# Ten gate tiles of the long sequence as seven-product Strassen groups in a stage of their own, and branch B's later queries and keys drawn over all units

## The chip, the cores and the metric

The kernel runs on one core of a Trainium2 chip, in one launch. The metric is the device time of that core in microseconds (us). Five engines work side by side, each through its own queue of instructions in a fixed order: PE (TensorE, matmuls, with PEld for its weight loads), DVE (VectorE), ACT (ScalarE), POOL (GpSimd), and SP, which only issues DMAs. An instruction that has to wait holds everything behind it on its engine.

## The reference

One layer of an encoder is computed for two inputs, a short one of 512 tokens and a long one of 1024 tokens, each of width 1024. In short:

```python
def _token_mixer(xn, w_in, q_norm_g, k_norm_g, rpb, w_proj_a, w_proj_b, w_out):
    z = xn @ w_in
    qa, ka, va, qb, kb, vb, ga, gb = jnp.split(z, idx, axis=-1)
    ...
    o_a = _gqa_attention(qa, ka, va)
    o_b = _neighbourhood_attention(qb.reshape(...), kb.reshape(...), vb.reshape(...), rpb)
    merged = jax.nn.sigmoid(ga) * (o_a @ w_proj_a) + jax.nn.sigmoid(gb) * (o_b @ w_proj_b)
    return merged @ w_out

def _trunk(x, ...):
    h = h + _token_mixer(_rmsnorm(h, norm_mix_g[l]), ...)
    hn = _rmsnorm(h, norm_mlp_g[l])
    h = h + jnp.square(jax.nn.relu(hn @ w_mlp_up[l])) @ w_mlp_down[l]
    return _rmsnorm(h, norm_final_g)
```

`ga` and `gb` are the two gates, each 1024 columns wide; they are what the change computes in another way. Everything is fp32.

## The kernel before

A product of two fp32 matrices is made of three matmuls: each operand is split into a high part (a copy in the type fp32r, by ACT) and a low part (what is left, a subtraction by DVE), and `mm3` (lines 191 to 193) adds high by high, high by low and low by high. The function `run` goes through one sequence; it is called for the short one (NB = 1, one block of 512 tokens) and then for the long one (NB = 2). Names in the profile have buffer numbers left out; `s1` in a name of the program's order is the long sequence. After both comes the MLP, which the change leaves as it is.

`run` has these stages. For each of two groups g of four heads of branch A: the phase `phR`, which makes queries, keys and values, and the phase `phA`, attention over eight units (a head and a block of 512 queries). In a unit, for each of eight blocks `kc` of 128 keys, PE transposes four tiles of probabilities (`pTs`, line 722), ACT and DVE split them (`pths` line 727, `ptls` line 728), and PE adds them to the output (`os`, lines 698 and 699) two blocks later. Between these, `s_tile` makes the next unit's scores: two times two matmuls into `ss`, a maximum by DVE (`nms`, line 682), an exponential by ACT (`ps`, line 685), a reciprocal by DVE (line 687) and the scaling by POOL (line 688). Then the phase `phB`, branch B: 32 units (a head and a strip of columns), each of `s_unit` (scores `sbs`, the sum with the bias and the minimum by DVE in line 891, exponential, reciprocal, POOL's scaling in line 899), one unit later `t_unit` (transposes `ptbs`, their split), and one more later `v_unit` (`obs`). Then `phG` merges and projects.

The gates are work that can stand anywhere. The generator `gate` makes them in tiles of 128 columns: per tile and block of 512 tokens eight times `mm3`, then a tanh by ACT and a store to `zg` in memory. `fill.pull(n)` takes n steps (one `mm3` each) of whatever `fill` holds, and stands at many places of `phA` and `phB`. For the long sequence, four tiles of the first gate (columns 2304 on) are drawn in each of the two `phA`, with a step in six of eight `kc`, and all eight tiles of the second gate (columns 3328 on) in `phB`, with five or six steps a unit. In `phB`, `qkproj` makes queries and keys for two heads; those of the first pair stand ahead of the units, those of each later pair (96 matmuls) are made within the last two of every eight units.

What is written here is the program's order. A scheduler then sets the order on each engine within what the dependences allow, except where an instruction is kept in program order (`keep_in_program_order`). Buffers come from pools: `rawp` has three of 4 KB per partition for what is loaded or waits to be split, `s8r` eleven of 8 KB, `pmm` four PSUM banks and `pbig` two double ones. A new tile waits until the buffer that it gets was read for the last time.

Of the kernel before, what the change touches and what calls it, by code (L numbers as in the profile page):

```python
# [61 lines left out]
def encoder(ctx: ExitStack, tc: tile.TileContext, xs, outs, w):  # L62
# [316 lines left out]
    def run(tr, nxt, first):  # L379
# [89 lines left out]
        def load_v(g, alloc, pin=False):  # L469
            return load_cols(win, 1792 + 256 * g, 256, f"v{N}_{g}", alloc, pin)  # L470

        early = {}
        for g in range(2):
            with phase(f"phR{N}_{g}") as ph:
                xn_of = {}
                fresh = g == 0 and tr.ready < NT
# [105 lines left out]
                for tt in range(NT):  # L582
# [84 lines left out]
            with phase(f"phA{N}_{g}") as ph:  # L667
# [41 lines left out]
                for ui, u in enumerate(units):  # L709
                    h, qb = u  # L710
                    if first:
                        bias_row(g * 4 + ui)
                        if g == 0 and ui == 1:
                            early["a"] = load_a(1)
                        if g == 0 and ui == 2:
                            early["v"] = load_v(1, slot)
                    nxt_u = units[ui + 1] if ui + 1 < len(units) else None
                    sdone = 0
                    for kc in range(NT):
                        pt = mm(f"pT{N}_{g}_{h}_{qb}_{kc}")  # L720
                        for j in range(4):
                            nc.tensor.transpose(  # L722
                                pt[:, j * P : (j + 1) * P], PP[u, j][:, kc * P : (kc + 1) * P], ident
                            )
                        hi = ph.tile([P, 512], F32R, tag="pth", name=f"pth{N}_{g}_{h}_{qb}_{kc}", bufs=3)
                        lo = ph.tile([P, 512], F32R, tag="ptl", name=f"ptl{N}_{g}_{h}_{qb}_{kc}", bufs=3)
                        nc.scalar.activation(hi, pt, AF.Copy)  # L727
                        nc.vector.tensor_tensor(lo, pt, hi.bitcast(F32), op=ALU.subtract)  # L728
# [9 lines left out]
                fill.drain()  # L738
                for item in queue:
                    pv(*item)  # L740

        mA = {}
        wp_b = []
# [44 lines left out]
        with phase(f"phB{N}") as ph:  # L788
# [18 lines left out]
            def load_qk(pr):  # L807
# [2 lines left out]
                    load_cols(win, 1280 + pr * P, P, f"bk{N}_{pr}"),  # L810
                )

            def qkproj(pr, wqk, dest):
                wq, wk = wqk
                qT = slot([P, 2, T], F32R, f"qB{N}_{pr}")
# [2 lines left out]
                for tb in range(NB):  # L818
                    cs = slice(tb * 512, tb * 512 + 512)
                    pq = mm(f"pqb{N}_{pr}_{tb}")  # L820
                    for k in range(NC8):
                        mm3(pq, wq[k][0], wq[k][1], xh(tb, k), xl(tb, k), k == 0, k == NC8 - 1)
                        yield
                    for e in range(2):
                        hs = slice(64 * e, 64 * e + 64)
                        ls = slice(64 - 64 * e, 128 - 64 * e)

                        src = pq[hs].rearrange("p (r j c) -> p j r c", j=4, c=16)

                        def strip_view(s_):  # L830
                            return qT[s_, e, :].rearrange("p (j r c) -> p j r c", j=4, c=16)[
                                :, :, tb * 8 : tb * 8 + 8, :
                            ]

                        dst_h, dst_l = strip_view(hs), strip_view(ls)
                        nc.scalar.activation(dst_h, src, AF.Copy, scale=0.125)
                        for jj in range(4):
                            nc.vector.scalar_tensor_tensor(
                                dst_l[:, jj],
                                src[:, jj],  # L840
                                0.125,
                                dst_h[:, jj].bitcast(F32),
                                op0=ALU.mult,
                                op1=ALU.subtract,
                            )
# [4 lines left out]
                    for e in range(2):  # L850
                        hs = slice(64 * e, 64 * e + 64)
                        ls = slice(64 - 64 * e, 128 - 64 * e)
                        for os_ in (hs, ls):
                            nc.scalar.activation(kT[e][os_, 0, cs], pk[hs], AF.Copy)
                        for os_ in (hs, ls):
                            nc.vector.tensor_tensor(
                                kT[e][os_, 1, cs], pk[hs], kT[e][hs, 0, cs].bitcast(F32), op=ALU.subtract
                            )

            qk = {}  # L860
            def s_unit(u):
# [86 lines left out]
                    finish_o(o, nq, None, ph, f"B{nm}", (hi, lo, ps))  # L948

            prep(0)  # L950
            fill.add(gate(3328, zg[1]))
            wqk = load_qk(0)
            fill.pull(1)
            for _ in qkproj(0, wqk, qk):
                pass
# [3 lines left out]
            qp = None  # L959
            for i in range(n + LS + LV):  # L960
                if i < n - 8:
                    f = (5 if i < LS else 2 + i % 2) if NB == 1 else 5 + (i % 3 > 0)
                else:
                    f = 3 + i % 2 if NB == 1 else 7
                if i < n:
                    s_unit(units[i])
                    if units[i][1] == 1 and units[i][0] + 1 < 8:
                        prep(units[i][0] + 1)
                    if i % 8 == 6 and i + 2 < n:
# [4 lines left out]
                    if i % 8 == 7 and qp is not None:  # L974
# [11 lines left out]
                if i == n - 8:  # L986
                    fill.drain()
                    fill.add(pa)
                if i == 3:
                    wqk = load_qk(1)  # L990
                if qp is not None and NB == 2:
                    for _ in range(NC8):
                        next(qp)
                fill.pull(f - f // 2)
                if 0 <= i - LS - LV < n:
                    v_unit(units[i - LS - LV])
            fill.drain()


# [707 lines left out]
```

## Time and profile before

| what | value |
|---|---|
| time, median of 3 runs | 2174.46 us (2173.92 to 2176.43) |
| span of the profiled execution | 2172.2 us; its time with what lies around the span is not on the page |
| median run less that span | 2.3 us |
| granted TensorE clock, mean | 0.997 |
| long sequence, `phA` of g = 0 and of g = 1 | about 468 to 592 us and 664 to 788 us |
| long sequence, `phB` up to the last eight units | 790 to 1010 us |

Times of the trace count from the start of the span. The busy time of an engine in a stretch is given beside the number of instructions that lie in it; PE's matmuls overlap each other, so the time that one costs is read from how many fit into a stretch, not from its own duration. A row of groups gives the line, engine, operation, tiles and shapes, the count, and then the busy time in us, the mean duration in ns and the idle time before.

### The profile page before, as it was taken

How to read it: one execution, taken by the hardware profiler on the slowest of the kernel's cores; microseconds unless marked ns; L12 is line 12 of the kernel's file. 1: busy time of each engine (PE TensorE's matmuls, PEld its weight loads, DVE VectorE, ACT ScalarE, POOL GpSimd, SP SyncE). 2: the span in 40 equal slices, each digit the busy share in tenths (PEclk: the TensorE clock that was granted, in tenths of full speed). 3: DMA queues.
4: the chain of work that ended last, by engine and by line, in shares of the span. 5: the costliest groups of instructions: out<-in, count | busy, mean ns of one | idle time of the engine just before them, and what ended most of it. 6: DMA issues, size and time to landing. Idle time of an engine off the chain costs nothing. (4 is left out here: it accounts for less than half of the span.)

```text
span 2172.2 us, 32392 instructions
## 1 busy us (share of the span) xinstructions
PE 2135.6 (98%) x11162; PEld 1867.9 (86%) x11162; DVE 1456.1 (67%) x2837; ACT 1109.3 (51%) x2379; POOL 349.4 (16%) x458
## 2 busy tenths in 40 slices
PE   8999999999999999999999999999999999999998
PEld 7788778888898888888888899998999988888886
DVE  6675566777756754555772777778777777769663
ACT  5654553556645744545531466656556643433452
POOL 2232210433233313322300200003000000000000
PEclk9999999999999999999999999999999999999999
DMA  5436457620122132423464656568544799788551
GB/s 166 144 104 179 137 145 249 211 71 28 45 75 86 44 92 88 125 80 110 136 195 137 202 180 195 179 226 223 158 156 155 234 347 343 224 268 290 175 194 68
DMA packets 319773, 350.94 MB, mean 162 GB/s; under 512 B 31352, under 2 KB 255224, under 8 KB 319609
## 3 DMA queue, kind: packets, MB, share of 16 engines
q1 hardware_dynamic: 277927, 279.65, 41.4%
q10 hardware_dynamic: 36002, 52.19, 6.9%
q0 software_dynamic: 5680, 17.04, 2.7%
q8 instruction: 88, 1.44, 0.3%
q14 instruction: 76, 0.62, 0.1%
HBM read 264.85 MB, written 87.88 MB: 162 GB/s over the span
## 5 line engine op out<-in xcount | busy, mean ns | idle before, releaser
L192 PE MATMUL dn<-wd,ah 128*128 128x512 f32 x624 | 243.0, 389 | 0.0
L193 PE MATMUL dn<-wd,al 128*128 128x512 f32 x624 | 243.0, 389 | 0.0
L191 PE MATMUL dn<-wd,ah 128*128 128x512 f32 x624 | 243.0, 389 | 0.0
L1184 ACT ACTIVATE ah<-ar 128x512 fp32r<-128x512 f32 x168 | 103.9, 627 | 195.1 <-PE dn L192 176.8
L1185 DVE TENSOR_TENSOR al<-ar,ah 128x512 fp32r<-128x512 f32 x168 | 115.1, 693 | 73.9 <-ACT ah L1184 66.7
L192 PEld LDWEIGHTS dn<-wd,ah 128*128 128x128 f32 x624 | 117.2, 188 | 24.4
L193 PEld LDWEIGHTS dn<-wd,al 128*128 128x128 f32 x624 | 117.2, 188 | 24.2
L191 PEld LDWEIGHTS dn<-wd,ah 128*128 128x128 f32 x624 | 117.2, 188 | 24.1
L728 DVE TENSOR_TENSOR ptls<-pTs,pths 128x512 fp32r<-128x512 f32 x160 | 107.7, 686 | 37.9 <-ACT pths L727 37.0
L727 ACT ACTIVATE pths<-pTs 128x512 fp32r<-128x512 f32 x160 | 94.1, 597 | 74.0 <-PE pTs L722 71.8
L688 POOL TENSOR_SCALAR ps<-ps,rls 128x1024 f32<-128x1024 f32 (+1 forms) x96 | 96.6, 1007 | 216.2 <-DVE rls L687 197.2
L682 DVE TENSOR_REDUCE nms<-ss 128x1 f32<-128x1024 f32 (+1 forms) x96 | 99.9, 1041 | 25.4 <-PE ss L680 25.0
L191 PE MATMUL gpss<-xs_0h,w_gs 128*128 128x512 f32 x256 | 106.2, 415 | 0.8 <-DVE rlbs L898 0.7
L685 ACT ACTIVATE ps<-ss,nms 128x1024 f32<-128x1024 f32 (+1 forms) x96 | 93.2, 972 | 22.4 <-DVE nms L682 20.0
L722 PEld LDWEIGHTS pTs<-ident,ps 128*128 128x128 f32 x640 | 78.2, 140 | 28.1 <-POOL ps L688 4.2
L193 PE MATMUL gpss<-xs_0h,w_gs 128*128 128x512 f32 x256 | 101.7, 397 | 0.0
L192 PE MATMUL gpss<-xs_0l,w_gs 128*128 128x512 f32 x256 | 101.6, 397 | 0.0
L722 PE MATMUL pTs<-ident,ps 128*128 128x128 f32 x640 | 98.9, 274 | 1.3 <-DVE ptls L728 0.6
L176 POOL TENSOR_TENSOR rs_f<-ms_f,mhalf 128x1 f32<-128x1 f32 x6 | 4.0, 667 | 590.7 <-DVE ms_f L172 590.7
L1184 ACT ACTIVATE A<-S 128x512 fp32r<-128x512 f32 x128 | 75.9, 623 | 29.4 <-DVE S L1247 22.1
L891 DVE CUSTOM_DVE_ANT_0 sbss<-sbs,bms 128x384 f32<-128x384 f32 (+1 forms) x96 | 48.6, 508 | 58.2 <-issue 34.1
L191 PE MATMUL ud<-B,A 128*128 128x384 f32 x256 | 85.8, 335 | 1.4 <-DVE c L1302 1.4
(325 smaller groups left out, 6444.8 us busy)
## 6 DMA issues: line engine op xcount, KB each, us to landing
ar<-ud SPq DMA_DIRECT2D x120, 512.0 KB
br<-in_w_mlp_down_dram SPq DMA_DIRECT2D x72, 512.0 KB
rawu<-in_w_mlp_up_dram SPq DMA_DIRECT2D x64, 512.0 KB
ud<-c ACTq DMA_DIRECT2D x128, 192.0 KB
raw_gs<-in_w_in_dram SPq DMA_DIRECT2D x32, 512.0 KB
zgs<-sgs ACTq DMA_DIRECT2D x48, 256.0 KB
ud<-cs SPq DMA_DIRECT2D x64, 192.0 KB
raw_os<-in_w_out_dram SPq DMA_DIRECT2D x16, 512.0 KB
```

Of the source, the lines that this page charges most:

```text
L191: nc.tensor.matmul(out, ah, bh, start=start, stop=False, **kw)
L192: nc.tensor.matmul(out, ah, bl, start=False, stop=False, **kw)
L193: nc.tensor.matmul(out, al, bh, start=False, stop=stop, **kw)
L682: nc.vector.tensor_reduce(nm_, s, axis=AX.X, op=ALU.max, negate=True)
L685: nc.scalar.activation(p, s, AF.Exp, bias=nm_, accum_out=l)
L688: nc.gpsimd.tensor_scalar(p, p, rl, 1.0, op0=ALU.mult, op1=ALU.mult)
L722: nc.tensor.transpose(pt[:, j * P : (j + 1) * P], PP[u, j][:, kc * P : (kc + 1) * P], ident)
L727: nc.scalar.activation(hi, pt, AF.Copy)
L728: nc.vector.tensor_tensor(lo, pt, hi.bitcast(F32), op=ALU.subtract)
L891: nc.vector.tensor_tensor_reduce(out=sb, in0=so, in1=bm, op0=ALU.add, op1=ALU.min, scale=-1.0, scalar=3e38, accum_out=nm_)
L1184: nc.scalar.activation(hi, src, AF.Copy)
L1185: nc.vector.tensor_tensor(lo, src, hi.bitcast(F32), op=ALU.subtract)
```

## The change

Three things are changed, all for the long sequence alone.

First, ten of the sixteen gate tiles go into a stage `wide` (phase `phS`) between the second `phA` and `phB`. They are taken as five groups of two tiles. A group is a product of a 1024 x 256 piece of the weights and the 1024 x 1024 input, cut into two by two blocks each, and made by Strassen's scheme (Winograd's form) of seven block products instead of eight; a block product is twelve matmuls of 128x512. Each group needs sums and differences of its weight blocks (`forms`), and all groups share sums and differences of the input's blocks (`x_forms`: numbers 2, 1, 3 and 6 are new; 0, 4, 5 and 7 are the input's own tiles). The new ones are made in 16 parts of 128x512 (`chunk`): POOL subtracts the low halves, DVE the high halves, POOL adds the two, and in a later step (`rest`) ACT makes the high part and DVE the low part. Of the 16 parts, seven stand in units 0 to 6 of the second `phA`, five in unit 7, four in `wide`.

Second, six gate tiles stay with `gate`: two in the first `phA` (a step in two of eight `kc`), three in the second (three of eight `kc`), one in `phB`.

Third, `qkproj2` makes the queries and keys of the pairs 1 to 3 in steps drawn over all eight units before they are needed (`nqp` steps a unit), with its weights asked for earlier.

```diff
+        def x_forms():
+            (h1, l1), (h2, l2) = tr.xhl[0], tr.xhl[1]
+            XF[0], XF[5], XF[4], XF[7] = (h1[0], l1[0]), (h1[1], l1[1]), (h2[1], l2[1]), (h2[0], l2[0])
+            def chunk(i, a, b, c):
...
+                hi, lo = (t[:, c, :] for t in XF[i])
+                (ah, al), (bh, bl) = ([t[:, c, :].bitcast(F32) for t in XF[n]] for n in (a, b))
+                de = rawp.tile([P, 2, 512], F32, tag="raw", name=f"xd{N}_{i}_{c}")
+                pin = tc.keep_in_program_order
+                pin(nc.gpsimd.tensor_tensor(de[:, 1], al, bl, op=ALU.subtract))
+                pin(nc.vector.tensor_tensor(de[:, 0], ah, bh, op=ALU.subtract))
+                pin(nc.gpsimd.tensor_tensor(de[:, 0], de[:, 0], de[:, 1], op=ALU.add))
+                def rest():
+                    pin(nc.scalar.activation(hi, de[:, 0], AF.Copy))
+                    pin(nc.vector.tensor_tensor(lo, de[:, 0], hi.bitcast(F32), op=ALU.subtract))
+                x_rest.append(rest)
+            for i, a, b in ((2, 7, 0), (1, 4, 2), (3, 4, 7), (6, 5, 1)):
+                x_todo.extend(partial(chunk, i, a, b, c) for c in range(4))
...
+        def wide(ph):
+            todo = [(2304 + i * P, i, zg[0]) for i in (4, 6)] + [(3328 + i * P, i, zg[1]) for i in (2, 4, 6)]
...
+                def prod(out, i, more):
+                    for k in range(4):
+                        mm3(out, A[i][:, 0, k, :], A[i][:, 1, k, :], XF[i][0][:, k, :], XF[i][1][:, k, :], ...)
...
+            ask(0)
+            side = forms(0, A)
+            ask(1)
+            for s in side[:3]:
+                s()
+            x_form_step()
+            for s in side[3:]:
+                s()
+            x_form_step()
+            fill.drain()
+            for n in range(len(todo)):
...
+                group(n, A, side)
+                A = nA
+                ask(n + 2)
...
-                        fill.add(gate(2304, zg[0], g * 4, g * 4 + 4))
+                        if NB == 1:
+                            fill.add(gate(2304, zg[0], g * 4, g * 4 + 4))
+                        else:
+                            fill.add(gate(2304, zg[0], g * 2, g * 2 + 2))
+                            if g == 1:
+                                fill.add(gate(3328, zg[1], 0, 1))
...
-                        fill.pull(1 if NB == 1 or kc % 4 < 3 else 0)
+                        fill.pull(1 if NB == 1 or kc % (4 - g) == 0 else 0)
+                        if NB == 2 and g == 1:
+                            if ui < 7:
+                                if kc == 6:
+                                    x_form_step()
+                                if kc == 1 and x_rest:
+                                    x_rest.pop(0)()
+                            elif kc % 2 == 1 or kc == 0:
+                                x_form_step()
...
+        if NB == 2:
+            with phase(f"phS{N}") as ph:
+                wide(ph)
...
+                nqp = (2, 4, 5, 5, 4, 4, 4, 4)[t8] if NB == 2 and i < n - 8 else 0
                 if i < n - 8:
-                    f = (5 if i < LS else 2 + i % 2) if NB == 1 else 5 + (i % 3 > 0)
+                    f = (5 if i < LS else 2 + i % 2) if NB == 1 else (4 if i < 2 else 2)
...
+                for _ in range(nqp // 2):
+                    next(qp, None)
                 fill.pull(f // 2)
                 if 0 <= i - LS < n:
                     t_unit(units[i - LS])
```

What the change does to the order is shown at three places. The first is DVE in the last unit (head 3, block 1) of the long sequence's second `phA`; `ptls` are the low parts that the output's matmuls wait for. Before:

```order
L728 TENSOR_TENSOR ptls1_1_3_1_2_9143<-pTs1_1_3_1_2_9137,pths1_1_3_1_2_9142 128x512
L728 TENSOR_TENSOR ptls1_1_3_1_3_9158<-pTs1_1_3_1_3_9152,pths1_1_3_1_3_9157 128x512
L728 TENSOR_TENSOR ptls1_1_3_1_4_9169<-pTs1_1_3_1_4_9163,pths1_1_3_1_4_9168 128x512
L728 TENSOR_TENSOR ptls1_1_3_1_5_9183<-pTs1_1_3_1_5_9177,pths1_1_3_1_5_9182 128x512
L728 TENSOR_TENSOR ptls1_1_3_1_6_9197<-pTs1_1_3_1_6_9191,pths1_1_3_1_6_9196 128x512
L728 TENSOR_TENSOR ptls1_1_3_1_7_9211<-pTs1_1_3_1_7_9205,pths1_1_3_1_7_9210 128x512
```

And now, with `xds` the differences (line 487) and `xfls` the low parts (line 492) of the new input forms, whose high parts and sums come from ACT and POOL:

```order
L492 TENSOR_TENSOR xfls1_3_8972<-xds1_3_0_8973,xfhs1_3_8971 128x512
L487 TENSOR_TENSOR xds1_3_1_9010<-xs1_1h1_4989,xs1_1h0_4988 128x512
L895 TENSOR_TENSOR ptls1_1_3_1_4_9022<-pTs1_1_3_1_4_9016,pths1_1_3_1_4_9021 128x512
L895 TENSOR_TENSOR ptls1_1_3_1_5_9033<-pTs1_1_3_1_5_9027,pths1_1_3_1_5_9032 128x512
L492 TENSOR_TENSOR xfls1_3_8972<-xds1_3_1_9010,xfhs1_3_8971 128x512
L487 TENSOR_TENSOR xds1_3_2_9038<-xs1_1h1_4989,xs1_1h0_4988 128x512
L895 TENSOR_TENSOR ptls1_1_3_1_6_9050<-pTs1_1_3_1_6_9044,pths1_1_3_1_6_9049 128x512
L895 TENSOR_TENSOR ptls1_1_3_1_7_9064<-pTs1_1_3_1_7_9058,pths1_1_3_1_7_9063 128x512
L492 TENSOR_TENSOR xfls1_3_8972<-xds1_3_2_9038,xfhs1_3_8971 128x512
L487 TENSOR_TENSOR xds1_3_3_9069<-xs1_1h1_4989,xs1_1h0_4988 128x512
```

Two instructions of a form now stand ahead of every two `ptls`, and the first of them needs POOL's and ACT's part of the same form.

The second place is POOL from the last unit on. Before, its last scaling of branch A is followed by branch B's mask and bias sums:

```order
L688 TENSOR_SCALAR ps1_1_3_1_2_9026<-ps1_1_3_1_2_9026,rls1_1_3_1_2_9029 128x1024
L688 TENSOR_SCALAR ps1_1_3_1_3_9050<-ps1_1_3_1_3_9050,rls1_1_3_1_3_9053 128x1024
L790 DMA msks1_9238<-in_mask2_dram 128x2304
L874 TENSOR_TENSOR bms1_0_1_0_9417<-rects1_0_9240,msks1_9238 128x384
L874 TENSOR_TENSOR bms1_0_1_1_9430<-rects1_0_9240,msks1_9238 128x384
```

Now ten parts of the input's forms (number 1 from its third part, then 3 and 6), two instructions each, stand between them; the first seven rows:

```order
L855 TENSOR_SCALAR ps1_1_3_1_3_8892<-ps1_1_3_1_3_8892,rls1_1_3_1_3_8895 128x1024
L486 TENSOR_TENSOR xds1_1_2_8923<-xs1_1l1_4991,xfls1_2_7943 128x512
L488 TENSOR_TENSOR xds1_1_2_8923<-xds1_1_2_8923 128x512
L486 TENSOR_TENSOR xds1_1_3_8954<-xs1_1l1_4991,xfls1_2_7943 128x512
L488 TENSOR_TENSOR xds1_1_3_8954<-xds1_1_3_8954 128x512
L486 TENSOR_TENSOR xds1_3_0_8973<-xs1_1l1_4991,xs1_1l0_4990 128x512
L488 TENSOR_TENSOR xds1_3_0_8973<-xds1_3_0_8973 128x512
```

POOL's addition of a part (line 488) waits for DVE's subtraction of the same part, and all ten follow each other.

The third place is SP, where the weights of the new stage are asked for. Before, single gate tiles followed head 0's values for branch B:

```order
L801 DMA vss1_0_9242<-vds1_4732 32x4x128 x16
L216 DMA raw_bqs1_0_0_9259<-in_w_in_dram 128x8x128
L216 DMA raw_bks1_0_0_9265<-in_w_in_dram 128x8x128
L216 DMA raw_gs1_3328_0_0_9271<-in_w_in_dram 128x8x128
L216 DMA raw_gs1_3328_1_0_9462<-in_w_in_dram 128x8x128
```

Now the groups' weights `rawss` stand first, and those values between them:

```order
L216 DMA raw_gs1_3328_0_0_8797<-in_w_in_dram 128x8x128
L519 DMA rawss1_0_0_9088<-in_w_in_dram 128x4x256
L519 DMA rawss1_0_1_9090<-in_w_in_dram 128x4x256
L519 DMA rawss1_1_0_9092<-in_w_in_dram 128x4x256
L519 DMA rawss1_1_1_9094<-in_w_in_dram 128x4x256
L981 DMA vss1_0_9850<-vds1_4732 32x4x128 x12
L519 DMA rawss1_2_0_9325<-in_w_in_dram 128x4x256
```

The two halves of group 0 (`rawss1_0_0`, `rawss1_0_1`) share the pool `rawp` with the parts `xds`; in the built program they get the buffers of the parts 1 and 2 of form 3, and all four parts of form 6 get, one after the other, the buffer of `rawss1_0_1`.

More of the change, by code (lines that the diff above doesn't have):

```diff
@@ L823, in qkproj @@
                         yield
[L824 to L845, printed above, removed]
+                    put_q(qT, pq, tb)
                     pk = mm(f"pkb{N}_{pr}_{tb}")
@@ L950, in run @@
             prep(0)
[L951 to L955, printed above, removed]
+            if NB == 1:
+                fill.add(gate(3328, zg[1]))
+                wqk = load_qk(0)
+                fill.pull(1)
+                for _ in qkproj(0, wqk, qk):
+                    pass
+            else:
+                raws = ask_qk(0)
+                wts = [cut_qk(raws, f"{i}_0") for i in range(2)]
+                fill.add(gate(3328, zg[1], 1, 2))
+                fill.pull(1)
+                raws = ask_qk(1)
+                for _ in qkproj2(0, wts, qk):
+                    pass
+                wts = [cut_qk(raws, "0_1")]
+                qp = qkproj2(1, wts, qk)
             units = [(h, j) for h in range(8) for j in (1, 2, 0, 3)]
@@ L973, in run @@
                             next(qp)
-                    if i % 8 == 7 and qp is not None:
+                    if i % 8 == 7 and qp is not None and NB == 1:
                         for _ in qp:
@@ L988, in run @@
                     fill.add(pa)
-                if i == 3:
+                if i == 3 and NB == 1:
                     wqk = load_qk(1)
-                if qp is not None and NB == 2:
-                    for _ in range(NC8):
-                        next(qp)
+                for _ in range(nqp - nqp // 2):
+                    next(qp, None)
                 fill.pull(f - f // 2)
```

202 lines of the change are left out of this document (190 added, 12 removed).

## The prediction

> **What bounds the kernel now.** First I read the page's busy times, to see which engine sets the span:
>
> ```profile
> span 2172.2 us, 32392 instructions
> PE 2135.6 (98%) x11162; PEld 1867.9 (86%) x11162; DVE 1456.1 (67%) x2837; ACT 1109.3 (51%) x2379; POOL 349.4 (16%) x458
> ```
>
> PE is busy nearly always, so fewer matmuls should be time, if PE stays that full where they go and where the filling work leaves. So the second view is the windows of the stages that change (both `phA` of the long sequence, then `phB`), and a dense one for the price of a matmul:
>
> ```profile
> core 0: us, PE busy (x) PEld busy (x) DVE busy (x) ACT busy (x) POOL busy (x), PEclk, DMA share, GB/s
> 468.00:592.00 124.00, 123.56 (x661) 100.71 (x660) 90.44 (x144) 81.69 (x145) 36.74 (x32) 1.00 0.13 39
> 664.00:788.00 124.00, 123.91 (x667) 101.28 (x666) 90.72 (x143) 82.72 (x144) 36.63 (x32) 1.00 0.17 48
> 812.00:1010.00 198.00, 195.41 (x1008) 162.97 (x1007) 100.20 (x290) 96.84 (x216) 59.78 (x82) 1.00 0.33 99
> ...
> 1900.00:2000.00 100.00, 100.00 (x443) 82.88 (x442) 76.08 (x102) 34.04 (x58) 0.00 (x0) 1.00 0.84 277
> ```
>
> In `phA` PE misses 0.4 and 0.1 us of 124, in `phB` 2.6 of 198. The last row, all of it 128x512 matmuls of the MLP, fits 441 starts (443 less two that reach over its edges) into 100 us: 0.227 us each. DVE, with 90 of 124 us in `phA`, is next in line.
>
> Third, the groups of DVE and ACT in the second `phA` (670 to 788 us):
>
> ```profile
> L728 DVE TENSOR_TENSOR ptls<-pTs,pths 128x512 fp32r<-128x512 f32 x63 | 42.2, 687 | 15.8 <-ACT pths L727 15.5
> L727 ACT ACTIVATE pths<-pTs 128x512 fp32r<-128x512 f32 x63 | 36.9, 597 | 29.0 <-PE pTs L722 28.1 <-ACT ps L685 0.2
> ```
>
> The column behind the mean shows that DVE waits for PE's work here, not the reverse.
>
> **The change part by part.** The sum is made on the profiled span of 2172.2 us; the median run is 2.3 us above it, and that stays.
>
> *Products.* Ten tiles of 48 matmuls (480) become five groups of 84 (420). 60 x 0.227 = 13.6 us less on PE, which bounds every stage they leave. This is the only saving. The stage itself is 420 x 0.227 = 95.3 us.
>
> *Weights, stores, copies of the groups.* Ten loads of 512 KB become ten of 512 KB, 20 tanh and stores stay 20. Per group DVE gets 16 instructions of 128x512 (4 sums, 7 low parts, 5 on results), at 0.69 us 11.0 of the group's 19.1 us. The cover is PE's own products: nothing, from the second group on. On SP the 16 loads of head 0's values now stand among the groups' loads; those are asked for a group ahead: nothing.
>
> *First `phA`.* A unit takes 124/8 = 15.5 us; four steps fewer take 12 x 0.227 = 2.7 away: 12.8. DVE needs 90.4/8 = 11.3. PE still bounds, but with 1.5 us to spare a unit instead of 4.2. Bounds 0 and 3 us for all eight; I take 1, near the lower end, since DVE stays under PE.
>
> *Second `phA`, units 0 to 6.* PE's unit falls by 9 x 0.227 = 2.0 to 13.5. DVE's rises by two instructions of a part, 11.3 + 2 x 0.69 = 12.7. And there is a hold, which a part of the MLP shows: line 327 runs the same kind of subtraction, both inputs in SBUF, on DVE and on POOL. Its groups (shortest, median, longest in ns), and then DVE's and POOL's timeline at 1211 us:
>
> ```profile
> L327 DVE TENSOR_TENSOR B<-ta,B x12: 678/694/1709, 1211.7 to 1500.3; 128x512 fp32r<-128x512 f32 x12
> L327 POOL TENSOR_TENSOR B<-ta,B x12: 1277/1294/1622, 1211.9 to 1500.1; 128x512 fp32r<-128x512 f32 x12
> ```
>
> ```profile
> 1211.69 2.39 DVE L327 TENSOR_TENSOR B<-ta,B 128x512 fp32r<-128x512 f32 x2
> ...
> 1211.91 1.62 POOL L327 TENSOR_TENSOR B<-ta,B 128x512 fp32r<-128x512 f32 x1 [2.85 <-DMA hn<-hnd]
> ```
>
> POOL's takes 1.29 us, DVE's 0.69 alone; where they meet, whoever comes second waits for the other's end (two on DVE 2.39 us instead of 1.4; POOL 1.62). In a part of the new forms POOL's and DVE's subtractions are issued together, so DVE stands up to 1709 - 694 = 1.0 us longer, with the `ptls` behind it: 13.7 us a unit against PE's 13.5. Bounds: 0 (the wait falls into PE's other work) and 1.0 + 0.2 a unit, 8 us for seven. I take 3, 0.4 a unit, because the surplus of the rows is 0.2 and neither engine can be kept wholly full.
>
> *Unit 7 and the start of `wide`: the term that decides.* Here parts no longer come one a unit but follow each other, and the last ones are needed. I count a chain from POOL's last scaling of the unit, which both the unit's first transposes and POOL's part 3 of form 1 wait for. First sum: 1.29 + 0.69 (held) + 1.29 = 3.3 us. Four more parts: POOL 1.29, DVE's low part of the part before and its own subtraction 2 x 0.69, POOL 1.29 = 4.0 each, 16.0: at 19.3 the sum of part 3 of form 3 stands. ACT 0.60 and DVE 0.69 free its buffer for the second half of group 0's weights: 20.6. That load is 512 KB; the nearest row with a landing time is a store of the same size (last column, us from issue to landing), 2.9:
>
> ```profile
> hnd<-xnhs POOLq DMA_DIRECT2D x8, 512.0 KB, 2.9
> ```
>
> At 23.5 DVE can start `S0`, first in its queue, then the low part of the first weight: 24.9, the first product. Ten DVE instructions later (6.9: 31.8) the weights release the one buffer of form 6, whose four parts go through it one by one: 1.29 + 0.69 + 1.29 + 0.60 + 0.69 = 4.6 each, 18.2: 50.0 us. PE's own work up to the product that needs form 6 is less. Its prices, from the timeline of PE:
>
> ```profile
> 710.00 0.40 PE L699 MATMUL os<-ptls,vhls 128*128 128x512 f32 x1
> 710.23 0.60 PE L722 MATMUL pTs<-ident,ps 128*128 128x128 f32 x4
> 710.59 0.48 PE L679 MATMUL ss<-kTs,qTs 128*128 128x512 f32 x1
> ```
>
> Start to start, four transposes take 0.36, an output matmul 0.23. Eight fours 2.9, 18 output matmuls 4.1, the 38 gate matmuls that the order has there 8.6, and 97 matmuls of `wide` up to the end of that product 22.0: 37.6. Loss 50.0 - 37.6 = 12. Without the hold the cycles are 3.3 instead of 4.0 and a part of form 6 takes 3.9: 43.7, loss 6. Bounds: 0 (the forms keep ahead of PE) and 17 (eight of group 0's own DVE instructions, 0.69 each, fall between the parts of form 6 on top of 12). I take 12, since rows of this trace show the hold whole.
>
> *Branch B.* Rows of `phB` from 812 to 1010 us, one of each engine in a unit's chain, and PE's wait at a new pair (us in total, times, longest):
>
> ```profile
> L891 DVE CUSTOM_DVE_ANT_0 sbss<-sbs,bms 128x384 f32<-128x384 f32 x47 | 26.0, 555 | 47.1 <-issue 31.4 <-PE sbs L888 15.6
> L896 ACT ACTIVATE pbs<-sbss,nmbs 128x384 f32<-128x384 f32 x47 | 28.9, 615 | 29.1 <-DVE nmbs L891 21.3 <-DVE rlbs L898 6.1 <-DVE os_Bs L428 1.0
> L899 POOL TENSOR_SCALAR pbs<-pbs,rlbs 128x384 f32<-128x384 f32 x47 | 27.2, 587 | 68.8 <-DVE rlbs L898 62.7 <-PE ptbs L911 6.1
> ```
>
> ```profile
> PE sbs L888 <- DVE kBs L856: 1.3, 2, 0.8
> ```
>
> 47 halves are 23.5 units: 8.4 us each. Seven gate tiles leave, 336 x 0.227 = 76 us: (198 - 76)/23.5 = 5.2 us of PE a unit, against DVE's 100.2/23.5 = 4.3. The chain of a half, 0.56 + 0.62 + 0.59 = 1.8 us, fits into the unit that lies between scores and transposes, so PE still bounds. What goes is the cover where a pair changes and the scores wait for the keys' copies: three times. Bounds -2.6 (all idle of the stage gone) and +6 (three times the two waits' 1.3, and as much again for thinner cover at other places); I take 1, near the row of 1.3.
>
> *The clock.* Idle PE can cost more than its idle time. Windows before and at the two falls of the granted clock (column behind POOL's):
>
> ```profile
> 256.00:260.00 4.00, 1.79 (x10) 1.32 (x10) 3.94 (x8) 3.38 (x8) 0.00 (x0) 1.00 0.28 80
> 260.00:263.50 3.50, 3.23 (x10) 2.69 (x10) 1.96 (x11) 1.48 (x6) 2.27 (x4) 0.51 0.47 154
> 408.00:413.70 5.70, 3.96 (x30) 3.67 (x29) 4.08 (x14) 5.03 (x35) 1.80 (x3) 1.00 0.85 265
> 413.70:417.20 3.50, 3.41 (x13) 2.90 (x12) 2.30 (x8) 1.58 (x7) 2.83 (x5) 0.52 0.42 135
> ```
>
> After 4 us with 1.79 busy, and after 5.7 with 3.96, the clock stands at about half for 3.5 us: 1.7 us of work lost. The waits of unit 7 and before `wide` are of that size. Bounds 0 and 3.4 (two falls); I take one, 1.7. [...]
>
> *Sum.* -13.6 + 1 + 3 + 12 + 1 + 1.7 = +5.1: span 2177.3, median 2179.6 us, slower by 0.23%. A measurement of this kernel tells 0.2% (4.3 us) from no change.
>
> **The rivals.**
> *Faster: the forms stay ahead.* If the chain of 50.0 us ends within PE's 37.6, that term and the clock's are 0: -13.6 + 1 + 3 + 1 = -8.6, 2165.9. For it: POOL has only 36.6 of 124 us to do in `phA`, and DVE's waits there are for PE. Against: ten parts in a row cost POOL alone 20 x 1.29 = 25.8, each with DVE and ACT between. It decides at 12 us off the chain; up to 4 us off (a chain of 46) the kernel isn't faster by what can be told.
> *No change: the hold is rare.* DVE and POOL miss each other, the chain is 43.7 (loss 6), the second `phA` loses 1 and the clock falls once: -13.6 + 1 + 1 + 6 + 1 + 1.7 = -2.9, 2171.6. For it: in the median of both rows of line 327 no hold is seen. Against: POOL's and DVE's subtractions of one part start on the same release.
> *Slower still: branch B starves.* With 4 steps instead of 5 or 6 and no dense pairs, PE waits 0.4 us a unit in 24 units: 10 on top, 2189.6. For it: DVE comes to 4.3 of 5.2 us. Against: the chain is 1.8 us.
> That the saving itself fails is no rival: the order of the changed kernel has the 420 matmuls, in the form whose price is read.
>
> **How the numbers follow.** Forecast 0.42, forms ahead 0.22, hold rare 0.29, B starving 0.07. Slower by over 0.2%: 0.42 + 0.07 = 0.49; within it: 0.29; faster: 0.22. The range reaches from the faster rival to the starving one: 2165 to 2191. The forecast's own case, with the chain's loss from 10 to 17 and `phA`'s from 2 to 8, goes from 2176 to 2190.
>
> **What would show each step.** Products: 420 matmuls of `wide` at 0.227 us. Second `phA`: about 111 us (8 x 13.5 and 3) up to its last unit, DVE there over 90% busy. Chain: in the last unit and the first product group, PE idle 12 us in total, its waits named by `ptls`, `xfls` or `sas`; DVE rows of lines 487 and 492 near 1.7 us where they meet lines 486 and 488; the first product 25 us after the last scaling. Clock: one stretch near 0.5 there. Branch B: idle as before, 2 to 4 us. The prediction is wrong if PE's waits at the forms of the input are under 4 us in all, or if `phA` with a third of its steps leaves PE waiting by more than 8 us.

## The result: slower by 0.9%, above the range

The changed kernel takes 2194.16 us (median of 4 runs, 2193.25 to 2198.0) against 2174.64 us; the ratio is 1.0093, 95% interval 1.0079 to 1.0108. That is 19.5 us slower, where 5.1 was forecast, and 3 us above the range's end. The profiled execution grew by 20.3 us:

```profile
span 2192.5 us, 32488 instructions
PE 2132.7 (97%) x11102; PEld 1854.1 (85%) x11102; DVE 1519.2 (69%) x2929; ACT 1135.2 (52%) x2430; POOL 398.0 (18%) x490
```

PE's matmuls are 60 fewer, yet its busy time falls by 2.9 us only: a matmul of 128x512, 0.39 us among others, counts 0.50 us at 776.3 us, after a wait of 1.7, and 0.63 from 804.7 us on, at a granted clock of 0.50. The windows of the changed stages (units 0 to 5 of the second `phA`; its units 6 and 7 and the first product group up to its last product; that product and the other groups; branch B):

```profile
core 0: us, PE busy (x) PEld busy (x) DVE busy (x) ACT busy (x) POOL busy (x), PEclk, DMA share, GB/s
643.70:738.70 95.00, 92.85 (x500) 73.94 (x499) 79.24 (x125) 70.35 (x124) 49.41 (x40) 1.00 0.08 24
738.70:804.10 65.40, 50.10 (x228) 37.71 (x226) 52.75 (x72) 31.07 (x56) 33.27 (x24) 0.93 0.22 67
804.10:883.80 79.70, 79.37 (x335) 64.05 (x336) 41.47 (x64) 31.23 (x51) 0.64 (x1) 0.97 0.47 145
907.40:1047.10 139.70, 134.56 (x745) 111.84 (x745) 101.17 (x302) 90.39 (x211) 64.01 (x84) 1.00 0.37 107
```

The hole is the second row: 15 of 65 us without a matmul, and the granted clock at 0.93.

To add up, I count PE's loss in a stretch: the time between two of its matmuls, less the number of matmuls of each kind times its dense price (0.2275 us for 512 columns, 0.1735 for 384, 0.12 for 256, 0.11 for 128; in the trace before, two in a row of one width start 0.227, 0.173, 0.120 and 0.109 us apart in the median). In us:

```
stretch                                       before  changed  more  predicted
first phA                                       3.0     5.1    2.1      1
second phA to the first output of unit 6        2.4     5.7    3.3      3 (unit 6 included)
from there to the end of the groups             0.3    23.8   23.5     13.7 (12 and the clock's 1.7)
branch B with its first queries and keys       11.6    15.9    4.3      1
ahead of the first phA (chance)                                0.6      0
```

Together 33.8, less 13.6 saved, is 20.2, the 20.3 but for rounding. PE's waits in the third stretch:

```profile
PE wds L191 <- DVE s5s L560: 8.4, 1, 8.4
PE pTs L889 <- DVE ptls L895: 1.9, 3, 1.1
PE os L865 <- DVE ptls L895: 1.8, 1, 1.8
PE was L193 <- DVE sas L550: 1.7, 1, 1.7
```

The longest is named by `s5s`: DVE still has to read the bank that the product of form 6 adds to. That read stands in DVE's queue between the parts of form 6. DVE and POOL just ahead of the release:

```profile
798.99 1.65 POOL L486 TENSOR_TENSOR xds<-xs_0l,xfls 128x512 f32<-128x512 f32 x1 [1.47 <-DVE xfls L492]
799.43 1.76 DVE L487 TENSOR_TENSOR xds<-xs_0h,xfhs 128x512 f32<-128x512 f32 x1
...
801.33 1.58 POOL L488 TENSOR_TENSOR xds<-xds 128x512 f32<-128x512 f32 x1 [0.69 <-DVE xds L487]
801.71 1.74 DVE L550 TENSOR_TENSOR sas<-rawss,sas 128x512 fp32r<-128x512 f32 x1
...
803.38 0.68 DVE L560 TENSOR_TENSOR s5s<-wds,s5s 128x512 f32<-128x512 f32 x1
...
803.98 0.68 DVE L492 TENSOR_TENSOR xfls<-xds,xfhs 128x512 fp32r<-128x512 f32 x1
...
804.11 0.80 PE L191 MATMUL wds<-xfhs,sas 128*128 128x512 f32 x1 [8.36 <-DVE s5s L560]
```

DVE is busy 7.2 of PE's 8.4 us of waiting, and two of these instructions take 1.75 us instead of 0.68, each beside one of POOL's. The last low part of form 6 ends at 804.7 us, but only the last three of the product's twelve matmuls need it: the parts of the first nine were there by 798.9 us. It is `s5s` that kept these from starting.

### The profile page after: what moved, and what is told of

It is laid out like the page before. It is cut to its first block, busy times and chain, and to the rows that moved or that the text cites. A ratio compares the mean times of both kernels' runs of the same rounds, so it can differ in the third digit from the quotient of the medians.

```text
span 2192.5 us, 32488 instructions
## 1 busy us (share of the span) xinstructions
PE 2132.7 (97%) x11102; PEld 1854.1 (85%) x11102; DVE 1519.2 (69%) x2929; ACT 1135.2 (52%) x2430; POOL 398.0 (18%) x490
## 5 line engine op out<-in xcount | busy, mean ns | idle before, releaser
L193 PEld LDWEIGHTS dn<-wd,al 128*128 128x128 f32 x624 | 117.2, 188 | 24.4
L852 ACT ACTIVATE ps<-ss,nms 128x1024 f32<-128x1024 f32 (+1 forms) x96 | 93.2, 971 | 18.2 <-DVE nms L849 17.6
L1124 POOL TENSOR_SCALAR pbs<-pbs,rlbs 128x384 f32<-128x384 f32 (+1 forms) x96 | 59.0, 619 | 163.4 <-DVE rlbs L1123 141.7
L1437 DVE TENSOR_TENSOR A<-S,A 128x512 fp32r<-128x512 f32 x128 | 84.5, 686 | 3.9 <-ACT A L1436 3.9
L1555 ACT ACTIVATE c<-c 128x384 f32<-128x384 f32 x96 | 50.3, 524 | 69.5 <-DVE c L1554 69.4
L191 PE MATMUL uc<-B,A 128*128 128x384 f32 x256 | 85.7, 335 | 0.0
```

Of the source, the lines that this page charges most:

```text
L191: nc.tensor.matmul(out, ah, bh, start=start, stop=False, **kw)
L193: nc.tensor.matmul(out, al, bh, start=False, stop=stop, **kw)
L852: nc.scalar.activation(p, s, AF.Exp, bias=nm_, accum_out=l)
L1124: nc.gpsimd.tensor_scalar(p, p, rl, 1.0, op0=ALU.mult, op1=ALU.mult)
L1437: nc.vector.tensor_tensor(lo, src, hi.bitcast(F32), op=ALU.subtract)
```

## The experiments

All are edits of the changed kernel; `qk_only` is edited back to the kernel before in all but one part. The table gives PE's loss in us in units 0 to 5 of the second `phA`, and from unit 6 to the end of the groups, the time, and the ratio to the kernel before.

```
kernel       units 0-5  unit 6 to end  median   ratio, 95% interval
changed         5.7        23.8        2194.2   1.0093 (1.0079 to 1.0108)
no_forms        2.7         4.3        2170.8   0.9982 (0.9973 to 0.9992)
dve_forms       9.7        13.8        2188.2   1.0058 (1.0043 to 1.0073)
spread         11.0        14.4        2192.2   1.0075 (1.0060 to 1.0090)
spread_dve     27.1        14.7        2205.9   1.0143 (1.0126 to 1.0160)
sg6             5.7        20.4        2191.9   1.0079 (1.0062 to 1.0096)
cover4          5.7        20.9        2196.0   1.0095 (1.0080 to 1.0110)
pool_forms      5.4        28.2        2198.4   1.0105 (1.0090 to 1.0120)
no_pool         5.2         7.1        2177.9   1.0016 (1.0007 to 1.0026)
no_dve          3.2        12.6        2181.2   1.0032 (1.0021 to 1.0044)
pool_aside      6.0        24.3        2195.7   1.0097 (1.0076 to 1.0117)
act_round       5.0         9.9        2181.3   1.0030 (1.0021 to 1.0040)
mix             5.8        14.0        2186.3   1.0055 (1.0040 to 1.0070)
mix_sg6         5.7        13.0        2185.0   1.0047 (1.0032 to 1.0062)
qk_only         2.5         0.3        2176.3   1.0008 (0.9999 to 1.0017)
```

**What do the forms cost?** `no_forms`:

```diff
-            for i, a, b in ((2, 7, 0), (1, 4, 2), (3, 4, 7), (6, 5, 1)):
-                x_todo.extend(partial(chunk, i, a, b, c) for c in range(4))
+            XF[2], XF[1], XF[3], XF[6] = XF[7], XF[4], XF[0], XF[5]
```

> Leaves out all 16 parts of the input's new forms (the products read the input's own tiles in their place, so the gates come out different); products, weights' sums, stores and order stay. In the trace of the changed kernel PE lost 23.5 us against dense work from the first output product of unit 6 of the second phA to the end of the product groups, 5.7 in the units before that, 5.1 in the first phA (before the change 0.4, 2.4 and 3.0 at the same places). Theory (the parts' chain through POOL, ACT and DVE is what PE waits for): the 23.5 fall to about 3, the 5.7 to about 5; 2173 us, 2170 to 2177. Rival cover (the thinner gate steps and the first weights' sums alone leave PE waiting): at least 12 of the 23.5 stay, 2183 or more.

As the theory had it: 2170.8. The 16 parts cost 23.4 us, more than all that the products save. The rival of the thin cover falls for this place: 4.3 us of the 23.8 stay, not 12.

**Whose work is it?** `dve_forms`, `spread` and `spread_dve`:

```diff
-                pin(nc.gpsimd.tensor_tensor(de[:, 1], al, bl, op=ALU.subtract))
+                pin(nc.vector.tensor_tensor(de[:, 1], al, bl, op=ALU.subtract))
...
-                pin(nc.gpsimd.tensor_tensor(de[:, 0], de[:, 0], de[:, 1], op=ALU.add))
+                pin(nc.vector.tensor_tensor(de[:, 0], de[:, 0], de[:, 1], op=ALU.add))
```

```diff
-                                if kc == 6:
+                                if kc == 2 or kc == 6:
                                     x_form_step()
-                                if kc == 1 and x_rest:
-                                    x_rest.pop(0)()
```

> POOL's two instructions of each part go to DVE, so a part is four instructions of DVE and one of ACT, with no handing over to POOL and no hold between POOL and DVE. Theory (chain): ten parts in a row took 3.83 us each where POOL takes part; on DVE alone a part is 4 x 0.61 = 2.4 and with its share of ptls about 3.1, and a part of form 6 about 3.2 instead of 5.3; the last part stands about 15 us earlier, PE's long wait of 8.4 us and the slow clock behind it go: 2182 us, 2178 to 2187. Rival work (DVE has too much to do, whoever does the rest): 32 instructions x 0.61 = 20 us more on DVE, less the holds: slower than the changed kernel, 2198 or more.

> Two parts a unit instead of one in units 0 to 6 of the second phA, so two are left for unit 7 and none for the stage of the products. Form 6 still has to wait for a buffer of the queries that is read last by the scores of unit 7. Theory (chain): 12 parts lie beside the units at some 0.5 to 1 us each more for PE's units, form 6 is complete before the first product group needs it: gains 23.5 - 8 and loses 5, 2184 us, 2178 to 2189. Rival work: DVE, 12.0 to 12.9 of 14 us busy in these units, is over full with a second part (14.4 or more), and the loss only moves forward: 2192 or more.

> Both at once: two parts a unit, all on DVE. DVE's unit would be 11.3 + 8 x 0.61 = 16.2 less what the fewer weight copies save (about 0.7), against PE's 13.5. Theory (chain): the units 0 to 6 become DVE's, 2 us longer each, 14 in all; unit 7 and the products lose only about 4: 2187 us, 2182 to 2193, worse than DVE alone without the spreading. Rival work: the same place pays more: 2198 or more.

`dve_forms` gained 6.0 us, neither the theory's 12 nor the rival's loss: the end got 10 better, the units 4 worse. `spread` gained 2.0, as little as the rival said: the end got 9 better, the units lost 5.3 of it. In `spread_dve` DVE is full, and the units are its own:

```profile
640.60:757.00 116.40, 101.09 (x501) 75.66 (x498) 105.43 (x161) 72.71 (x131) 40.63 (x28) 0.97 0.07 20
```

With 105.4 of 116.4 us on DVE, 12 parts cost 24.4 us: 2.0 each, about the four instructions of 0.6 (in `pool_aside` DVE's of 128x512 start 0.60 us apart from 805.43 to 806.63 us). So where DVE is full its work counts; at the end, where 10 parts on DVE alone cost less than with POOL, it is something else.

**Is it the buffer, or missing cover?** `sg6` and `cover4`:

```diff
+                if i == 6 and c % 2 == 0:
+                    d0, d1 = (sgp.tile([P, 512], F32, tag="sg", ...) for n_ in "ab")
```

```diff
-... for i in (4, 6)] + [(3328 + i * P, i, zg[1]) for i in (2, 4, 6)]
+... for i in (4, 6)] + [(3328 + i * P, i, zg[1]) for i in (2, 4)]
+            g6 = gate(3328, zg[1], 6, 7)
+            next(g6)
+            fill.add(g6)
             ask(0)
...
                 fill.add(gate(3328, zg[1], 1, 2))
+                fill.add(gate(3328, zg[1], 7, 8))
```

> The first and third part of form 6 get two small buffers of the gates' outputs, which stand free there, instead of the buffer of group 0's second weights; so the first needs no longer wait for that buffer (783 us in the changed kernel, while POOL was free from 773 us), and two parts can be under way. All else stays. Theory (chain of handing over, in series through one buffer): form 6 is complete some 10 us earlier, PE's wait of 8.4 us shrinks to 1 or less and the slow clock behind it (2.2 us) goes: 2185 us, 2181 to 2188. Rival work: DVE is busy 25.8 of the 30.8 us from the first product to form 6's end, so the end can come at most 5 us earlier: 2189 to 2193.

> Four groups instead of five; of the two gate tiles of the fifth one stands as 48 plain matmuls (10.9 us) ahead of the first product, the other in branch B. Costs 12 matmuls more, 2.7 us. Theory (the parts' chain has a length of its own, 52.5 us from POOL's last scaling of unit 7 to the last part, whatever PE does): PE's waits at the first weights (1.7) and at form 6 (8.4) and the slow clock (2.2) are covered, 12.3 less 2.7: 2184.5 us, 2181 to 2189. Rival work (DVE can't do more per time, so that what is put ahead only moves the wait): 2192 or more.

Both misses for the theory. `sg6` gained 2.2 us, as the rival's bound allowed. `cover4` gained nothing for its 10.9 us of cover. PE's waits there, from the first product on:

```profile
PE was L191 <- ACT s1s L587: 2.6, 1, 2.6
PE wcs L191 <- ACT s5s L594: 2.4, 1, 2.4
PE w0s L191 <- ACT s1s L587: 1.7, 1, 1.7
```

`s1s` and `s5s` are plain copies of finished products; they stand in ACT's queue behind the high parts of form 6 (before the first one ACT idles 2.8 us for POOL's sum, with `s1s` next in its queue). The cover also moved the chain itself: POOL begins form 6 at 787.2 us instead of 783.3. So the parts do not run beside the products: in queues of fixed order they hold up the products' own instructions, and plain matmuls put ahead only move that.

**Which share of a part?** `pool_forms` (DVE's first instruction to POOL), `no_pool` and `no_dve`:

```diff
-                pin(nc.vector.tensor_tensor(de[:, 0], ah, bh, op=ALU.subtract))
+                pin(nc.gpsimd.tensor_tensor(de[:, 0], ah, bh, op=ALU.subtract))
```

```diff
-                pin(nc.gpsimd.tensor_tensor(de[:, 1], al, bl, op=ALU.subtract))
                 pin(nc.vector.tensor_tensor(de[:, 0], ah, bh, op=ALU.subtract))
-                pin(nc.gpsimd.tensor_tensor(de[:, 0], de[:, 0], de[:, 1], op=ALU.add))
```

```diff
-                pin(nc.vector.tensor_tensor(de[:, 0], ah, bh, op=ALU.subtract))
-                pin(nc.gpsimd.tensor_tensor(de[:, 0], de[:, 0], de[:, 1], op=ALU.add))
+                pin(nc.gpsimd.tensor_tensor(de[:, 0], ah, de[:, 1], op=ALU.add))
...
-                    pin(nc.vector.tensor_tensor(lo, de[:, 0], hi.bitcast(F32), op=ALU.subtract))
+                    pin(nc.scalar.activation(lo, de[:, 1], AF.Copy))
```

> DVE's subtraction of a part goes to POOL: DVE keeps one instruction of a part (the low part), POOL has three (3 x 1.29 = 3.9 us). Units 0 to 5 of the second phA lost 3.0 us more with the parts than without. Theory (in the units DVE's share of a part is what PE pays; at the end the chain): 6 x 0.61 us less on DVE, so 1 to 1.5 of the 3.0 are left, unit 6 gets 1 to 2 better; the row of ten parts stays as long (3.9 a part): 2191 us, 2187 to 2194. Rival hold (each of POOL's instructions holds DVE, and there are 16 more): 2195 to 2200.

> Leaves out POOL's two instructions of each part (the input's low halves stay out of the new forms); DVE's two and ACT's one stay, in the same order and buffers. The forms cost 23.4 us in the changed kernel (2194.2 against 2170.8 without any). Theory interplay (POOL and DVE hold each other and hand each part over twice, which makes a part 3.8 to 5.3 us long at the end): most goes, 8 us of the 23.4 or less stay, 2176 us, 2173 to 2179. Rival work (DVE's own 32 instructions are what PE pays): 14 or more stay, 2185 or more.

> The other half: leaves out DVE's two instructions of each part. POOL keeps two (its second adds a high half to its first result), ACT makes the high part and, in DVE's place, a copy of POOL's first result as the low part; order and buffers stay. Theory interplay: with nothing handed over to DVE little stays, 8 us of the 23.4 or less, 2176 us, 2172 to 2179. Rival POOL (the row of POOL's instructions and their holds on DVE's other work): 14 or more stay, 2185 or more. If this and the kernel without POOL's part each keep about half, the cost is plain work, which adds up, and not interplay.

`pool_forms` went as the rival hold said: more on POOL, 4 us slower. `no_pool` went as its theory said; `no_dve` lies between its theory and its rival. In the units nearly all of the parts' 3.0 us stays with DVE's two instructions (2.5) and little with POOL's (0.5). It isn't DVE's time alone, though: `pool_forms` takes one of the two from DVE, and 2.7 stay. At the end, of 19.5 us (23.8 less 4.3), DVE's share alone leaves 2.8 and POOL's alone 8.3: 8.4 come only when both are there.

**Hold or handing over?** `pool_aside` and `act_round`:

```diff
-                pin(nc.gpsimd.tensor_tensor(de[:, 0], de[:, 0], de[:, 1], op=ALU.add))
+                pin(nc.gpsimd.tensor_tensor(de[:, 1], de[:, 1], al, op=ALU.add))
```

```diff
-                pin(nc.gpsimd.tensor_tensor(de[:, 1], al, bl, op=ALU.subtract))
+                pin(nc.scalar.activation(de[:, 1], al, AF.Copy))
...
-                pin(nc.gpsimd.tensor_tensor(de[:, 0], de[:, 0], de[:, 1], op=ALU.add))
+                pin(nc.scalar.activation(de[:, 0], de[:, 0], AF.Copy))
```

> POOL does both its instructions of each part at the same places and on the same buffers, but its second adds to its own half, so that neither DVE nor ACT waits for it: the handing over goes, POOL's work and its holds on DVE stay. The new forms lack the input's low halves. From unit 6 of the second phA to the end of the groups PE lost 23.8 us in the changed kernel, 7.1 without POOL's instructions, 4.3 without any forms. Theory handing over (POOL to ACT to DVE to POOL in queues of fixed order): 10 or less of the 23.8 stay, 2180 us or less. Rival hold (POOL's instructions lengthen DVE's from 0.7 to 1.1 and 1.75 us): 16 or more stay, 2187 or more.

> The reverse: POOL's two instructions of a part become two copies by ACT at the same places (0.6 us each instead of 1.3; the forms lack the input's low halves), so DVE, ACT and DVE still wait for each other in turn, and POOL holds nobody. Theory handing over: the rounds stay, though each is shorter by about a quarter (two of its four steps fall from 1.3 to 0.6 us): 12 or more of the 23.8 us stay, 2183 us or more. Rival hold: as without POOL's instructions, 7 to 9 stay, 2177 to 2180.

In the main the hold. Without the handing over but with POOL's instructions the end loses 24.3, as much as before; with the handing over but without POOL 9.9, a little more than the hold's range (2181.3 us where 2180 was its end). PE's wait for `s5s`, 8.4 us in the changed kernel, is 5.7 in `pool_aside`, and 0.7 in `act_round` and in `no_pool`. And the hold can be added up: from unit 6 through group 0, what DVE's additions and subtractions of 128x512 took above 0.69 us each is 9.0 us in the changed kernel, 12.5 in `pool_aside`, 0.7 in `act_round` and 0.4 in `no_pool`.

How much the handing over costs stays open. In `pool_aside` there is more hold than before, which may hide what the handing over gave back, and the one buffer of form 6 still ties POOL and DVE together; in `act_round` the rounds are shorter (ACT's copies take 0.63 us, POOL's instructions 1.29), and a part of the 9.9 may be handing over.

The rows of group 0's weights show that the hold strikes work that has nothing to do with the parts. Low parts of the weights in the changed kernel, and in `no_pool`; and the low parts of `phA`, with one input in PSUM, in the changed kernel:

```profile
L550 DVE TENSOR_TENSOR sas<-rawss,sas x9: 679/683/1765, 775.5 to 809.9; 128x512 fp32r<-128x512 f32 x9
```

```profile
L548 DVE TENSOR_TENSOR sas<-rawss,sas x10: 679/684/694, 763.8 to 797.6; 128x512 fp32r<-128x512 f32 x10
```

```profile
L895 DVE TENSOR_TENSOR ptls<-pTs,pths x64: 666/679/692, 658.3 to 768.5; 128x512 fp32r<-128x512 f32 x64
```

The rows give its size: up to 1765 ns in the changed kernel against 694 at most without POOL's instructions, and no change with a PSUM input, 692 at most, though 47 of these 64 ran beside one of POOL's. The timeline of DVE and POOL above also shows until when it lasts: DVE's two long instructions end 0.55 and 0.54 us after the one of POOL's beside them (801.19 after 800.64 us, 803.45 after 802.91).

**A better version?** `mix` has POOL only where the units hide it; `mix_sg6` adds the buffers:

```diff
+                eng = nc.gpsimd if i in (2,) or (i == 1 and c < 2) else nc.vector
-                pin(nc.gpsimd.tensor_tensor(de[:, 1], al, bl, op=ALU.subtract))
+                pin(eng.tensor_tensor(de[:, 1], al, bl, op=ALU.subtract))
...
-                pin(nc.gpsimd.tensor_tensor(de[:, 0], de[:, 0], de[:, 1], op=ALU.add))
+                pin(eng.tensor_tensor(de[:, 0], de[:, 0], de[:, 1], op=ALU.add))
```

> The complete kernel again: the first six parts (units 0 to 5 of the second phA) with POOL as in the changed kernel, the ten others (unit 6 to the first group) all on DVE. In the traces the units before unit 6 lost 5.7 us with POOL and 9.7 with DVE alone, and from unit 6 to the end of the groups it was 23.8 with POOL and 13.8 with DVE alone. Theory (the two places are independent): 5.7 and 13.8, so 10 less than the changed kernel: 2184 us, 2181 to 2187. Rival (DVE's queue carries its delay from unit to unit): no better than all on DVE, 2187 or more.

> The same, with the gates' two small buffers for the first and third part of form 6. Theory (DVE is full there, back to back, so that buffers don't matter any more): as the kernel without them within 1.5 us, 2184. Rival buffer (the first part of form 6 still waits for group 0's weights): 3 us or more better, 2181 or less.

The two places are independent, as expected (5.8 and 14.0), and the buffers matter little then (1.3 us). `mix_sg6` is the best complete version, 9 us better than the changed kernel, and still 0.5% slower than before. With all forms free the change would gain 0.2%, so nothing here beats the kernel before clearly.

**Branch B.** `qk_only` keeps `qkproj2` alone: no groups, no forms, all sixteen gate tiles as before.

```diff
-        if NB == 2:
-            with phase(f"phS{N}") as ph:
-                wide(ph)
...
-                fill.add(gate(3328, zg[1], 1, 2))
+                fill.add(gate(3328, zg[1]))
...
-                    f = (5 if i < LS else 2 + i % 2) if NB == 1 else (4 if i < 2 else 2)
+                    f = (5 if i < LS else 2 + i % 2) if NB == 1 else 5 + (i % 3 > 0)
```

> The kernel before with the third part of the change alone: queries and keys of pairs 1 to 3 drawn over all units of branch B, all sixteen gate tiles as before. In branch B PE stood idle for 4.0 us before, most of it where a pair changes. Theory (thinner cover, not the spreading, makes branch B 3.9 us dearer in the changed kernel): part of the 4.0 goes, 2173.5 us, 2171 to 2176. Rival switching (more changes between kinds of matmuls cost PE): 2178 or more.

Between theory and rival, and not told from no change: 1.0008. By the trace branch B loses 13.4 instead of 11.6 us. So of the changed kernel's 4.3 some 1.8 come with the spreading, and the other 2.5 are left for the thinner cover, which no run has alone; the spreading does not help, as I had thought it would.

## Why the prediction was wrong

*Products: right.* With the forms gone the kernel is 0.2% faster than before (2170.8 against 2175.5 in the same comparison): 13.6 less some 9 that the thinner cover and the first weights take. Of these 9 the forecast had 2, for the first `phA` and branch B.

*The step that failed: unit 7 and the start of `wide`, 12 us with 0 to 17.* From the end of POOL's last scaling to the first matmul of form 6 it took 52.5 us (751.6 to 804.1), and PE's dense work in it is 35.3: a loss of 17.2, the slow clock's 1.7 in it, where 50.0 and 37.6 gave 12. Up to form 6 the chain was right: POOL began it 31.7 us after the scaling, 31.8 were predicted. Two things behind that were not.

First, the hold was named, but sized for the parts' own instructions alone (1.0 us once a part). It goes both ways and strikes other work too: beside form 6, four sums and low parts of the weights take 1.7 to 1.8 us on DVE instead of 0.7, and POOL's eight instructions 13.3 us instead of 10.3. The four parts took 21.4 us (783.3 to 804.7), not 18.2, and DVE's whole queue came late. Second, the 37.6 us of cover held the twelve matmuls of form 6's own product, 2.7 us. PE could do none of them meanwhile: their bank still had to be read by `s5s`, which stands in that queue. That also undid the step "weights, stores, copies: nothing".

Another 3.5 us come behind the chain, 2.2 of them the second fall of the clock, and 3.1 ahead of the scaling, 2.4 of them in unit 6.

*Clock: one fall of 1.7 predicted.* PE runs at about half speed in two places, the second and the last row:

```profile
752.00:757.20 5.20, 3.45 (x19) 2.40 (x17) 3.04 (x5) 2.91 (x5) 3.83 (x4) 1.00 0.00 0
757.20:760.90 3.70, 3.67 (x11) 3.03 (x12) 2.79 (x5) 1.23 (x2) 2.40 (x3) 0.54 0.15 35
...
804.00:808.50 4.50, 4.39 (x10) 3.48 (x11) 2.46 (x5) 2.76 (x6) 0.00 (x0) 0.50 0.74 213
```

That is 1.7 and 2.2 us of work, 3.9 in all and above the upper bound of 3.4. The first fall follows a wait of 1.8 us.

*Units 0 to 6: 5.7 against 3, within 0 to 8, but not for the stated reason.* Units 0 to 5 lose 3.3 more than before and unit 6 another 2.4. The reason was that the hold makes DVE's unit longer than PE's (13.7 us against 13.5). But in units 0 to 5 the holds add up to only 2.1 us, DVE is at 79.2 of 95.0 us (83%), not over 90%, and POOL's instructions by themselves keep only 0.5 us of loss.

*First `phA` and branch B: 2.1 and 4.3 against 1 and 1.* Within their bounds, but both came out on the upper side: each was taken near its lower end because PE or DVE had room on average. That room does not prevent waits within a unit, as POOL's scalings show, twice in the first `phA` (0.7 us) and three times in units 0 to 5 of the second:

```profile
PE pTs L889 <- POOL ps L855: 1.6, 3, 0.6
```

*The stated tests.* The first product's third matmul ran 24.7 us after the scaling's end (25 stated); PE stood idle 13.4 us from the scaling's end to form 6's product (12 in the last unit and the first group); lines 487 and 492 reached 1.78 and 1.31 us (1.7). PE's waits were to be named by `ptls`, `xfls` or `sas`: `ptls` and `sas` are there, `xfls` isn't, and the longest is `s5s`, which was not on the list. The falls of the clock were two, not one, and branch B's idle was 5.1 us in the window above, not 2 to 4. The rival that the hold is rare was the wrong way about: the runs without POOL's instructions show that it decides at the end.

## What to carry to other kernels

A helper's work on POOL was not free here, though POOL was busy for 18% of the span: DVE's SBUF-only instructions beside POOL's took 1.1 to 1.78 us instead of 0.68, and without POOL's part of the forms the kernel took 2177.9 us instead of 2194.2. So price each instruction of a helper by what it does to those beside it, those of other work included. Work that is pinned into queues of fixed order has to be followed to what stands behind it, copies of results above all; cover on PE didn't help against that here (`cover4`: 2196.0 us against 2194.2). And a saving on the bounding engine (13.6 us) has to be set against all that its cover had hidden: when the small terms of such a sum are all taken near their lower bounds because there is room on average, they come out too low together (here 5 for both `phA` and branch B, and 12 measured).

## What the runs showed of the hardware that I had not expected

In the 5.2 us up to 757.2 us PE was busy for 3.45 and waited at most 1.8 us at a time; in the next 3.7 us the granted clock was 0.54. From unit 6 through group 0, twelve of DVE's instructions of 128x512 with two SBUF inputs took 1.09 to 1.78 us, each beside one of POOL's, where such an instruction takes 0.68 without; the 64 low parts with a PSUM input took 0.67 to 0.69. And POOL's own, 1.29 us alone, took up to 1.80 beside DVE's.
